# Grouped-query attention on one core: the order model counts the array's switches, and K is turned first in a unit

## The chip, the core and the metric

The kernel runs on one core of a Trainium2 chip. A core has five engines that work side by side and meet through semaphores: TensorE (PE; its weight loads are shown as PEld), VectorE (DVE), ScalarE (ACT), GpSimd (POOL) and SyncE (SP). The metric is device time in microseconds (us), the median of several runs.

## What is computed

Attention in float32 with 8 batches, 512 positions, 32 query heads, 8 key/value heads and a head size of 64; four query heads share a key/value head.

```python
batch, seq, n_heads, n_kv_heads, dim = 8, 512, 32, 8, 64
K_expanded = np.repeat(K, heads_per_group, axis=2)   # also V
scores = np.einsum('bhqd,bhkd->bhqk', Q, K_expanded) * scale
weights = np.exp(scores - np.max(scores, axis=-1, keepdims=True))
weights = weights / (np.sum(weights, axis=-1, keepdims=True) + 1e-10)
output = np.einsum('bhqk,bhkd->bhqd', weights, V_expanded)
return output.transpose(0, 2, 1, 3).astype(np.float32)
```

## The kernel before

**Tiling.** The work is cut into 32 units: a batch and two key/value heads, so eight query heads. A unit has four pairs of query heads. The two heads of a pair use the upper and the lower 64 rows of the PE array at the same time: `mm_scores` (L229) makes, for a pair and a chunk of 128 keys, two matmuls of 64 rows each (the array is row-tiled then) into one PSUM tile of 128 x 1024. A pair has four such chunks. Three of them go to ACT, which takes the exponential (`exp_act`, L245; PSUM tiles `sa`, two buffers). The fourth (chunk 1, `DVE_KC`) goes to DVE, which makes the exponential by an integer trick in one instruction (`exp_dve`, L253; PSUM tile `sd`, one buffer). Both write bf16 weights into `pt`.

**Fills.** Everything else that PE does is a *fill*, and needs all 128 rows of the array. An `out` fill (`mm_out`, L263) multiplies weights by V, with a column of ones beside V that gives the sums: 4 matmuls of 65 columns a block of 128 queries, 7 or 4 blocks a fill. A `turn` fill (`mm_turn`, L322) transposes a unit's Q (two halves of 8) or K (4) on PE. All fills share two PSUM buffers `x`. DVE empties them: `take_out` (L279) copies into `raw`, and after a unit's last block takes the reciprocal of the sums (L303); POOL then divides (L305) and starts the store (L317). `take_turn` (L334) copies into `qt` or `kt`. K's two heads are needed in both halves of the partitions, so behind K's copy SP issues two DMAs that copy each half of `kt` across (L340, L341). The first score of a unit needs both.

**Loads.** POOL issues the loads of Q a unit (L206), and of K and V a batch (L213, L218), cast to bf16 on the way. It runs its own instructions in program order.

**Order.** Nothing is scheduled at run time. `Plan` walks through a model of PE, ACT and DVE with costs for each kind of work and writes down in which order PE and DVE issue theirs. At each step it has three candidates: the next ACT score (time `ta`), the next DVE score (`td`) and the next matmul of the next fill (`tf`). Before, an ACT score is taken when it can start within `LOOK` = 0.05, else a DVE score that can start now, else a fill. The list `fills` (L350 on) sets the order of the fills. In a unit before, they are: out 0, out 7, Q half 0, out 14, Q half 1, out 21, **K**, out 25 (the number is the first block); Q and K are those of two units later. The kernel then replays `plan.ops` (L430 on); loads of the next batch are issued when the scores reach pair 6 of a batch.

Of the kernel before, what the change touches and what calls it, by code (L numbers as in the profile page):

```python
# [19 lines left out]
NEVER = 1e9  # L20


class Plan:

    SCORE, SCORE_LAT = 0.222, 0.436
    BLOCK, TURN, X_LAT = 0.122, 0.056, 0.2
    EXP, EXP_VIS = 0.904, 1.077  # L30
    SCH, SCH_VIS = 1.14, 1.277
    LOOK = 0.05

    def __init__(self, npair, kcs, on_dve, fills, arrive, x_cost, nact, ndve, nx, npt, ahead):
# [5 lines left out]
        parts, x_free = {}, [0.0] * nx  # L40
        ready = []
        pe = act = dve = 0.0
        ia = id_ = fi = at = nxt = 0
        slot = 0

        def have(p):
            u, i = divmod(p, 4)
            return max(parts.get((u, None), NEVER), parts.get((u, i // 2), NEVER))

        def ring(free, issued, n):  # L50
            if issued < n:
                return 0.0
            return free[issued - n] if len(free) > issued - n else NEVER

        def score_at(q, i, free, n):
            if i >= len(q):
                return NEVER
            p = q[i][0]
            if p >= npt and p - npt not in pair_done:
                return NEVER  # L60
            return max(ring(free, i, n), have(p))
# [34 lines left out]
        parts[(0, None)] = parts[(0, 0)] = 0.0  # L96
        while True:
            run_dve(pe)
            ta = score_at(qa, ia, act_free, nact)
            td = score_at(qd, id_, dve_free, ndve)  # L100
            if td < NEVER and ia < len(qa):
                p, kc = qd[id_]
                if p * kcs + kc > qa[ia][0] * kcs + qa[ia][1] + ahead:
                    td = NEVER
            tf = fill_at()
            first = min(ta, td, tf)
            if first > pe and ready:
                soon = min(max(dve, j[0]) for j in ready)
                if soon < first and ta > pe + self.LOOK:
                    pe = max(pe, soon)  # L110
                    run_dve(pe)
                    continue
            if first >= NEVER:
                break
            if ta <= pe + self.LOOK or (first == ta and td > pe and tf > pe):
                pe = max(pe, ta)
                self.ops.append((pe, "pe", "act", qa[ia]))
                start = max(act, pe + self.SCORE_LAT)
                self.ops.append((start, "act", "score", qa[ia]))
                act = start + self.EXP  # L120
                act_free.append(start + self.EXP_VIS)
                pt_done[qa[ia]] = start + self.EXP_VIS
                ia += 1
                pe += self.SCORE
            elif td <= pe or (first == td and tf > pe):
                pe = max(pe, td)
                self.ops.append((pe, "pe", "dve", qd[id_]))
                ready.append((pe + self.SCORE_LAT, "score", qd[id_], None))
                id_ += 1
                pe += self.SCORE  # L130
            else:
                f = fills[fi]
                pe = max(pe, tf)
                self.ops.append((pe, "pe", f[0], (f, at)))
                pe += self.TURN if f[0] == "turn" else self.BLOCK
                if at == 0:
                    slot = nxt % nx
                    x_free[slot] = NEVER
                    nxt += 1
                at += 1  # L140
                if f[0] == "out" and (f[2] + at) % 8 == 0:
                    pair_done[f[1] * 4 + (f[2] + at) // 8 - 1] = pe
                if at == f[3]:
                    ready.append((pe + self.X_LAT, f[0], f, slot))
                    fi, at = fi + 1, 0
        assert ia == len(qa) and id_ == len(qd) and fi == len(fills) and not ready
        self.ops = [o for _, o in sorted(enumerate(self.ops), key=lambda e: (e[1][0], e[0]))]

# [2 lines left out]
def kernel(  # L151
# [14 lines left out]
    NU = B * GP  # L166
# [30 lines left out]
    score, xs = {}, {}  # L197
# [153 lines left out]
    for u in range(NU):  # L351
        if u == 0:
            fills += [("out", 0, 0, 7), ("out", 0, 7, 7), ("turn", 1, 1, 8)]
            fills += [("turn", 2, 0, 8), ("out", 0, 14, 7), ("turn", 2, 1, 8)]
            fills += [("out", 0, 21, 4), ("turn", 2, None, 4), ("out", 0, 25, 7)]
        elif u < NU - 1:
# [8 lines left out]
        else:  # L365
            fills += [("out", u, lo, 4) for lo in range(0, UB, 4)]

    def x_cost(f):
        if f[0] == "turn":
# [6 lines left out]
    def arrive(f):  # L376
        return {(0, 1): 2.0, (1, None): 4.0}.get(f[1:3], 5.0 if f[1] == 1 else 0.0)

    plan = Plan(
        NP, SC, lambda p, kc: kc == DVE_KC, fills, arrive, x_cost,  # L380
        nact=2, ndve=1, nx=2, npt=4, ahead=3,
    )

    with tc.manual_schedule(engines={PE, ACT, DVE, POOL, SP}):
# [45 lines left out]
        for _, engine, kind, what in plan.ops:  # L430
# [4 lines left out]
            elif engine == "pe":  # L435
                p, kc = what
# [42 lines left out]
```

## Time and profile before

| | |
|---|---|
| time, median of 3 runs | 409.66 us (409.02 to 410.01) |
| profiled execution, its own time | 408.85 us |
| its span, first to last instruction | 407.1 us |
| PE busy | 371.7 us (91%) |
| ACT busy | 367.6 us (90%) |
| DVE busy | 302.7 us (74%) |
| POOL busy | 193.0 us (47%) |
| chain that ended last, by engine | PE 65%, DVE 15%, DMA 12% |

Busy time of PE counts matmuls whose ends are modelled, so 91% does not say that PE works at its peak. PE and ACT are about equally busy; which of them holds up the other can't be read from the shares, only from the waits.

### The profile page before, as it was taken

The numbers are of one execution on the slowest core, as the hardware profiler recorded it, in microseconds if no ns is written. First come the engines' busy times: TensorE is split into PE (matmuls) and PEld (weight loads), VectorE is DVE, ScalarE is ACT, GpSimd is POOL, SyncE is SP. The second block draws the span as 40 slices with busy tenths as digits, with TensorE's granted clock in tenths as the row PEclk, the third lists the DMA queues.
The fourth block names the chain that finished last, engine by engine and source line by source line (L and its number), as shares of the span: only waits on it lengthen the run. The fifth ranks groups of instructions, "written<-read, shape, count | busy, mean of one in ns | idle before, by whom it ended". The sixth has DMA issues, their size and how long they took to land.

```text
span 407.1 us, 12995 instructions
## 1 busy us (share of the span) xinstructions
PE 371.7 (91%) x5764; PEld 225.7 (55%) x5764; DVE 302.7 (74%) x426; ACT 367.6 (90%) x387; POOL 193.0 (47%) x135
## 2 busy tenths in 40 slices
PE   4998999998999979999899989999899998999993
PEld 1454556655665535656456645655556564656552
DVE  3775778876787848878778767878678886888872
ACT  3897999997999949999899988999799998999993
POOL 7024544456544545445555652456643357444353
PEclk9998999998999969999999998999999999999998
DMA  9996167769367991678945597655967769422326
GB/s 183 212 177 161 41 163 169 170 157 239 84 134 171 191 236 39 147 169 185 242 131 147 136 202 178 151 147 146 199 146 171 168 149 245 121 68 99 119 105 208
DMA packets 41961, 64.15 MB, mean 158 GB/s; under 512 B 2352, under 2 KB 33968, under 8 KB 41904
## 3 DMA queue, kind: packets, MB, share of 16 engines
q0 software_dynamic: 33776, 57.41, 63.3%
q1 hardware_dynamic: 7600, 5.64, 5.3%
q8 instruction: 45, 0.74, 0.7%
q10 hardware_dynamic: 528, 0.26, 0.2%
q14 instruction: 12, 0.10, 0.1%
HBM read 50.59 MB, written 33.55 MB: 207 GB/s over the span
## 4 chain that ended last, share of the span: by engine, by line
PE 65%; DVE 15%; DMA 12%; issue 3%; ACT 3%; POOL 1%; DVEq 0%; POOLq 0%; ACTq 0%
PE x L270 27%; PE sa L236 22%; DMA kt<-kt 10%; PE x L332 9%; DVE pt L254 9%; PE sd L236 7%; DVE qt L346 4%; DMA q_nat<-in_Q_dram 3%; ACT pt L246 3%; DVE kt L339 1%; DVE raw L290 1%; POOL v_nat L218 0%; POOL q_nat L206 0%; DVEq L254 0%; POOL k_nat L213 0%
## 5 line engine op out<-in xcount | busy, mean ns | idle before, releaser
L246 ACT ACTIVATE pt<-sa 128x1024 bf16<-128x1024 f32 x384 | 365.1, 1029 | 28.1 <-PE sa L236 23.0
L254 DVE TENSOR_SCALAR pt<-sd 128x1024 uint16<-128x1024 f32 x128 | 156.4, 1222 | 70.2 <-PE sd L236 65.0
L305 POOL TENSOR_TENSOR o_sb<-raw,inv 128x2048 f32<-128x2048 f32 (+2 forms) x33 | 115.0, 3485 | 185.6 <-DVE inv L303 185.6
L270 PEld LDWEIGHTS <-pt 128*128 128x128 bf16 x4096 | 147.5, 98 | 63.2 <-issue 61.0
L236 PE MATMUL sa<-qt,kt 64*128 64x512 bf16 x768 | 153.0, 395 | 2.2 <-ACT pt L246 2.0
L290 DVE COPY raw<-x 128x455 f32<-128x455 f32 (+1 forms) x161 | 93.1, 578 | 20.4 <-PE x L270 20.3
L236 PEld LDWEIGHTS <-kt 64*128 64x128 bf16 x1024 | 41.7, 94 | 46.3 <-DMA kt<-kt 14.6
L236 PE MATMUL sd<-qt,kt 64*128 64x512 bf16 x256 | 53.9, 390 | 10.4 <-DMA kt<-kt 10.4
L332 PE MATMUL x<-ident,q_nat 128*128 128x128 bf16 x504 | 50.7, 227 | 0.5 <-DVE raw L290 0.4
L332 PEld LDWEIGHTS <-q_nat 128*128 128x128 bf16 x504 | 31.3, 100 | 33.6 <-issue 32.6
L346 DVE COPY qt<-x 128x1024 bf16<-128x1024 bf16 x63 | 43.0, 682 | 0.9 <-PE x L332 0.7
L317 POOL DMA_DIRECT2D out_dram<-o_sb x31 | 25.2, 813 | 9.3 <-POOL o_sb L305 9.3
L206 POOL DMA_DIRECT2D q_nat<-in_Q_dram x32 | 24.0, 753 | 10.3 <-PE x L332 9.9
L270 PE MATMUL x<-v_155,pt 128*128 128x65 bf16 x512 | 23.8, 197 | 1.5 <-DVE raw L290 1.5
L332 PE MATMUL x<-ident,k_nat 128*128 128x128 bf16 x124 | 16.8, 223 | 8.9 <-DVE qt L346 8.7
L332 PEld LDWEIGHTS <-k_nat 128*128 128x128 bf16 x124 | 9.2, 98 | 26.5 <-issue 26.4
L270 PE MATMUL x<-v_3822,pt 128*128 128x65 bf16 x512 | 23.2, 197 | 0.0
L270 PE MATMUL x<-v_1856,pt 128*128 128x65 bf16 x512 | 23.1, 197 | 0.0
L270 PE MATMUL x<-v_836,pt 128*128 128x65 bf16 x512 | 22.7, 196 | 0.0
L270 PE MATMUL x<-v_6771,pt 128*128 128x65 bf16 x512 | 21.8, 194 | 0.7 <-ACT pt L246 0.7
L270 PE MATMUL x<-v_5788,pt 128*128 128x65 bf16 x512 | 22.4, 194 | 0.0
L270 PE MATMUL x<-v_2839,pt 128*128 128x65 bf16 x512 | 22.4, 194 | 0.0
(42 smaller groups left out, 87.6 us busy)
## 6 DMA issues: line engine op xcount, KB each, us to landing
out_dram<-o_sb POOLq DMA_DIRECT2D x31, 1024.0 KB, 5.7
q_nat<-in_Q_dram POOLq DMA_DIRECT2D x31, 512.0 KB, 8.2
v_nat<-in_V_dram POOLq DMA_DIRECT2D x8, 512.0 KB, 10.8
k_nat<-in_K_dram POOLq DMA_DIRECT2D x8, 512.0 KB, 8.0
kt<-kt SPq DMA_DIRECT2D x62, 64.0 KB, 3.1
out_dram<-o_sb SPq DMA_DIRECT2D x1, 512.0 KB, 4.7
out_dram<-o_sb SPq DMA_DIRECT2D x2, 256.0 KB, 3.4
q_102<-in_Q_dram ACTq DMA_DIRECT2D x1, 256.0 KB, 4.3
```

Source lines behind the costliest of these rows:

```text
L206: nc.gpsimd.dma_start(out=t[:, :, lo * D:hi * D], in_=rows(Q, b, HU * gp + lo, HU * gp + hi))
L236: nc.tensor.matmul(s[:, m, :], kt[u][64 * m:64 * m + 64, 0 if m == g else 1, kc * 128:(kc + 1) * 128], qt[u][64 * m:64 * m + 64, i, :], st ...
L246: nc.scalar.activation(out=pts[p][:, kc, :, :], in_=score.pop((p, kc)), func=mybir.ActivationFunctionType.Exp, scale=float(scale),)
L254: nc.vector.tensor_scalar(out=pts[p][:, kc, :, :].bitcast(U16), in0=score.pop((p, kc)), scalar1=float(A_schr), scalar2=float(B_schr), op0= ...
L270: nc.tensor.matmul(xs[f][:, at * D1:(at + 1) * D1], pts[u * HPG + i][:, kc, m, qc * 128:(qc + 1) * 128], v1[u // GP][:, kc, 2 * (u % GP) + ...
L290: nc.vector.tensor_copy(out=raws[u][:, lo:lo + n, :], in_=x[:, 0:n * D1])
L305: eng.tensor_tensor(out=osbs[u].rearrange("p qc h d -> p h qc d")[:, lo // SC:lo // SC + nh], in0=src[:, :, 0:D].rearrange("p (h qc) d -> ...
L317: eng.dma_start(out=rows(out, b, HU * gp + h0, HU * gp + h1), in_=osbs[u][:, :, h0:h1, :].rearrange("p qc h d -> p qc (h d)"),)
L332: nc.tensor.transpose(xs[f][:, at * 128:(at + 1) * 128], src, ident)
L339: nc.vector.tensor_copy(out=k[:, 0, :], in_=x[:, 0:S])
L346: nc.vector.tensor_copy(out=qt[u][:, 2 * part:2 * part + 2, :], in_=x)
```

## The change

It has four parts.

1. `Plan` charges `DRAIN` = 0.1 whenever PE goes from scores to fills or back (the flag `scoring`).
2. A DVE score is taken only while PE is at scores already, that is right behind an ACT score or ahead of one; it comes to stand alone only when nothing else is left. `LOOK` becomes an argument and is 0.
3. In the model, the two DMAs behind K's copy take 4.0 instead of 2.5.
4. The fills of a unit are now: out 0, **K**, out 7, Q half 0, out 14, Q half 1, out 21, out 25.

```diff
-    LOOK = 0.05
+    DRAIN = 0.1
...
-                        parts[(j[2][1], j[2][2])] = start + vis + (2.5 if j[2][2] is None else 0.0)
+                        swap = 4.0 if j[2][2] is None else 0.0
+                        parts[(j[2][1], j[2][2])] = start + vis + swap
...
-            if ta <= pe + self.LOOK or (first == ta and td > pe and tf > pe):
...
-            elif td <= pe or (first == td and tf > pe):
...
+            if ta <= pe + look or (first == ta and not (scoring and td <= pe)):
+                kind = "act"
+            elif scoring and td <= pe:
+                kind = "dve"
+            elif tf <= pe or first == tf:
+                kind = "fill"
             else:
+                kind = "dve"
+            if kind == "fill":
                 f = fills[fi]
-                pe = max(pe, tf)
+                pe = max(pe + (self.DRAIN if scoring else 0.0), tf)
+                scoring = False
...
+            pe = max(pe + (0.0 if scoring else self.DRAIN), ta if kind == "act" else td)
+            scoring = True
...
+    LOOK = 0.0
...
-            fills += [("out", u, 0, 7), ("out", u, 7, 7)]
-            t = u + 2 < NU
-            fills += [("turn", u + 2, 0, 8)] if t else []
-            fills += [("out", u, 14, 7)]
-            fills += [("turn", u + 2, 1, 8)] if t else []
-            fills += [("out", u, 21, 4)]
-            fills += [("turn", u + 2, None, 4)] if t else []
-            fills += [("out", u, 25, 7)]
...
+        fills += [("out", u, 0, 7)]
+        fills += [("turn", u + 2, None, 4)] if t else []
+        fills += [("out", u, 7, 7)]
+        fills += [("turn", 1, 1, 8)] if u == 0 else []
+        fills += [("turn", u + 2, 0, 8)] if t else []
+        fills += [("out", u, 14, 7)]
+        fills += [("turn", u + 2, 1, 8)] if t else []
+        fills += [("out", u, 21, 4), ("out", u, 25, 7)]
```

What this makes of the order, at three places. First DVE, in the repeating unit, before (`raw` are output copies, 455 columns for 7 blocks and 260 for 4, `kt` and `qt` the copies of turned K and Q, TENSOR_SCALAR the exponential of a DVE score):

```order
L254 TENSOR_SCALAR pt<-sd 128x1024
L290 COPY raw<-x 128x455 x2
L254 TENSOR_SCALAR pt<-sd 128x1024
L346 COPY qt<-x 128x1024
L290 COPY raw<-x 128x455
L254 TENSOR_SCALAR pt<-sd 128x1024
L346 COPY qt<-x 128x1024
L290 COPY raw<-x 128x260
L254 TENSOR_SCALAR pt<-sd 128x1024
L339 COPY kt<-x 128x512
L290 COPY raw<-x 128x455
L303 RECIPROCAL inv<-raw 128x32
```

and the same unit of the changed kernel:

```order
L265 TENSOR_SCALAR pt<-sd 128x1024
L301 COPY raw<-x 128x455
L350 COPY kt<-x 128x512
L265 TENSOR_SCALAR pt<-sd 128x1024
L301 COPY raw<-x 128x455
L357 COPY qt<-x 128x1024
L265 TENSOR_SCALAR pt<-sd 128x1024
L301 COPY raw<-x 128x455
L357 COPY qt<-x 128x1024
L265 TENSOR_SCALAR pt<-sd 128x1024
L301 COPY raw<-x 128x260
L301 COPY raw<-x 128x455
```

K's copy has moved from the end of the unit to its second copy. Behind the last row of the changed unit follow the reciprocal (L314) and the next unit's exponential.

Second, PE in the repeating unit. Before, the DVE score (`sd`) stands behind one ACT score (`sa`); here it is the visit between the two halves of K's transposes:

```order
L332 MATMUL x<-ident,k_nat 128x128
L236 LDWEIGHTS kt
L236 MATMUL sa<-qt,kt 128x512
L236 LDWEIGHTS kt
L236 MATMUL sa<-qt,kt 128x512
L236 LDWEIGHTS kt
L236 MATMUL sd<-qt,kt 128x512
L236 LDWEIGHTS kt
L236 MATMUL sd<-qt,kt 128x512
L332 LDWEIGHTS k_nat
```

In the changed unit one visit to the scores holds an ACT, a DVE and another ACT score before the output matmuls go on:

```order
L247 LDWEIGHTS kt
L247 MATMUL sa<-qt,kt 128x512
L247 LDWEIGHTS kt
L247 MATMUL sa<-qt,kt 128x512
L247 LDWEIGHTS kt
L247 MATMUL sd<-qt,kt 128x512
L247 LDWEIGHTS kt
L247 MATMUL sd<-qt,kt 128x512
L247 LDWEIGHTS kt
L247 MATMUL sa<-qt,kt 128x512
L247 LDWEIGHTS kt
L247 MATMUL sa<-qt,kt 128x512
```

The unit has 12 visits before and 11 after, each between two runs of fills.

Third, POOL, where the loads of K and V of the next batch stand. Before:

```order
L206 DMA q_nat<-in_Q_dram 128x4x512
L305 TENSOR_TENSOR o_sb<-raw,inv 128x8x4x64
L317 DMA out_dram<-o_sb 128x4x512
L213 DMA k_nat<-in_K_dram 128x4x512
L218 DMA v_nat<-in_V_dram 128x4x512
L206 DMA q_nat<-in_Q_dram 128x4x512
```

and in the changed kernel:

```order
L217 DMA q_nat<-in_Q_dram 128x4x512
L224 DMA k_nat<-in_K_dram 128x4x512
L229 DMA v_nat<-in_V_dram 128x4x512
L316 TENSOR_TENSOR o_sb<-raw,inv 128x8x4x64
L328 DMA out_dram<-o_sb 128x4x512
L217 DMA q_nat<-in_Q_dram 128x4x512
```

The two loads have moved ahead of a unit's division and store, behind the Q load of the unit before. SP's order and ACT's are the same in both kernels but for line numbers.

More of the change, by code (lines that the diff above doesn't have):

```diff
@@ L31, with __init__ @@
     SCH, SCH_VIS = 1.14, 1.277
-    LOOK = 0.05
-    def __init__(self, npair, kcs, on_dve, fills, arrive, x_cost, nact, ndve, nx, npt, ahead):
+    DRAIN = 0.1
+    def __init__(self, npair, kcs, on_dve, fills, arrive, x_cost, nact, ndve, nx, npt, ahead, look):
         self.ops = []
@@ L60, in score_at @@
                 return NEVER
-            return max(ring(free, i, n), have(p))
+            u, j = divmod(p, 4)
+            return max(
+                ring(free, i, n), parts.get((u, None), NEVER), parts.get((u, j // 2), NEVER)
+            )
         def fill_at():
@@ L108, in __init__ @@
                 soon = min(max(dve, j[0]) for j in ready)
-                if soon < first and ta > pe + self.LOOK:
+                if soon < first and ta > pe + look:
                     pe = max(pe, soon)
@@ L114, in __init__ @@
                 break
-            if ta <= pe + self.LOOK or (first == ta and td > pe and tf > pe):
[L116 to L124, printed above, removed]
-            elif td <= pe or (first == td and tf > pe):
[L126 to L130, printed above, removed]
-            else:
+            if ta <= pe + look or (first == ta and not (scoring and td <= pe)):
[4 more added lines that the diff above has]
+                kind = "fill"
+            else:
+                kind = "dve"
+            if kind == "fill":
                 f = fills[fi]
-                pe = max(pe, tf)
+                pe = max(pe + (self.DRAIN if scoring else 0.0), tf)
+                scoring = False
                 self.ops.append((pe, "pe", f[0], (f, at)))
@@ L145, in __init__ @@
                     fi, at = fi + 1, 0
+                continue
+            pe = max(pe + (0.0 if scoring else self.DRAIN), ta if kind == "act" else td)
+            scoring = True
+            if kind == "act":
+                self.ops.append((pe, "pe", "act", qa[ia]))
+                start = max(act, pe + self.SCORE_LAT)
+                self.ops.append((start, "act", "score", qa[ia]))
+                act = start + self.EXP
+                act_free.append(start + self.EXP_VIS)
+                pt_done[qa[ia]] = start + self.EXP_VIS
+                ia += 1
+            else:
+                self.ops.append((pe, "pe", "dve", qd[id_]))
+                ready.append((pe + self.SCORE_LAT, "score", qd[id_], None))
+                id_ += 1
+            pe += self.SCORE
         assert ia == len(qa) and id_ == len(qd) and fi == len(fills) and not ready
@@ L350 @@
     fills = [("turn", 0, 1, 8), ("turn", 1, None, 4), ("turn", 1, 0, 8)]
[L351 to L356, printed above, removed]
[L357 to L366 removed]
+    for u in range(NU - 1):
+        t = u + 2 < NU
+        fills += [("out", u, 0, 7)]
[6 more added lines that the diff above has]
+        fills += [("out", u, 21, 4), ("out", u, 25, 7)]
+    fills += [("out", NU - 1, lo, 4) for lo in range(0, UB, 4)]
     def x_cost(f):
@@ L380 @@
         NP, SC, lambda p, kc: kc == DVE_KC, fills, arrive, x_cost,
-        nact=2, ndve=1, nx=2, npt=4, ahead=3,
+        nact=2, ndve=1, nx=2, npt=4, ahead=3, look=LOOK,
     )
```

6 lines of the change are left out of this document (1 added, 5 removed).

## The prediction

> **What bounds the kernel now.** I read first who waits for whom, ScalarE (ACT) first, because it has the most fixed work: 384 exponentials.
>
> ```profile
> ACT pt L246 <- PE sa L236: 23.0, 25, 4.0
> PEld L236 <- DMA kt<-kt: 14.6, 9, 3.2
> PE sd L236 <- DMA kt<-kt: 10.4, 7, 2.7
> PE x L332 <- DVE qt L346: 8.7, 25, 0.4
> ```
>
> Each row is waiter <- releaser: total us, times, longest. ACT is idle 23.0 us, always for scores from TensorE (PE). PE in turn waits for the small DMAs kt<-kt, which copy K's two halves across (I call them the swap), and 25 times, 0.35 us each, for a PSUM buffer x that VectorE (DVE) has yet to empty. Next I cut the ACT row by windows: 94 to 343 us, then 33 to 41 us. The last two fences have the first and last run of exponentials.
>
> ```profile
> ACT pt L246 <- PE sa L236: 16.0, 11, 4.0
> ```
> ```profile
> ACT pt L246 <- PE sa L236: 2.7, 4, 1.3
> ```
> ```profile
> 8.66 2.86 ACT L246 ACTIVATE pt<-sa 128x1024 bf16<-128x1024 f32 x3 [1.26 <-PE sa L236]
> ```
> ```profile
> 341.75 58.84 ACT L246 ACTIVATE pt<-sa 128x1024 bf16<-128x1024 f32 x62 [1.51 <-PE sa L236]
> ```
>
> So 16.0 us are lost in 11 gaps of the main stretch and 2.7 us in four early ones. One such place in the chain that ended last:
>
> ```profile
> 88.38 0.23 PE sd L236 x2
> ```
> ```profile
> 89.85 0.42 DVE kt L339
> 90.28 0.02 issue
> 90.30 5.35 DMA kt<-kt
> 95.65 0.05 issue
> 95.70 0.39 PE sd L236
> ```
> ```profile
> DMA to landing us min/median/max: 1.9/3.3/6.8
> ```
>
> K's transposes end near 88.6, DVE copies them at 89.85, the swap leaves at 90.30, takes 5.35 us, and PE stands until 95.70. Before, six ACT scores lie between the last transpose of a K and the first score that reads it: 6 x 0.957 = 5.7 us (0.957 is 11.49 / 12, below). Minus 1.7 us from transposes to swap (88.6 to 90.30), minus some 0.7 us by which a score runs ahead of its exponential, 3.3 us are left. The median swap takes 3.3 us and the slowest 6.8: it fits or misses by chance of the traffic.
>
> Between the stalls the pace is that of a repeating unit (4 pairs of heads, 12 ACT scores, 4 DVE scores). The same place of it in the chain, two units apart:
>
> ```profile
> 299.80 0.59 PE x L270 x16
> ...
> 322.79 0.60 PE x L270 x16
> ```
>
> 22.99 / 2 = 11.49 us. ACT alone needs less: in the row of 8.66 three exponentials take 2.86 us, and with 1.02 us for the last the step is 0.92 us, 12 x 0.92 = 11.04 a unit. So between stalls PE sets the pace, by its work and one x wait.
>
> **The change, part by part.** *PE's visits to the scores.* I price a visit from PE's own rows.
>
> ```profile
> 156.61 0.39 PE L236 MATMUL sa<-qt,kt 64*128 64x512 bf16 x2
> 156.84 0.38 PE L236 MATMUL sd<-qt,kt 64*128 64x512 bf16 x2
> 157.15 0.54 PE L270 MATMUL x<-v_1856,pt 128*128 128x65 bf16 x12
> 157.62 0.39 PE L236 MATMUL sa<-qt,kt 64*128 64x512 bf16 x2
> ```
> ```profile
> 157.94 0.90 PE L270 MATMUL x<-v_1856,pt 128*128 128x65 bf16 x24
> 158.77 0.39 PE L236 MATMUL sa<-qt,kt 64*128 64x512 bf16 x2
> ```
> ```profile
> 160.03 0.45 PE L332 MATMUL x<-ident,q_nat 128*128 128x128 bf16 x5
> 160.32 0.41 PE L270 MATMUL x<-v_1856,pt 128*128 128x65 bf16 x8
> 160.66 0.39 PE L236 MATMUL sa<-qt,kt 64*128 64x512 bf16 x2
> ```
>
> From start to start: a score alone 0.32 (157.62 to 157.94), two together 0.54 (156.61 to 157.15), so the second costs 0.22. Twelve output matmuls take 0.47 and 24 take 0.83: 0.03 each and 0.11 fixed. Five transposes and eight outputs take 0.63; minus 0.11 and 0.24, a transpose is 0.055. A visit to the scores thus costs 0.32 + 0.11 - 0.22 = 0.21 us beside its scores. Counted in the two orders, the visits fall from 384 to 351. Only eight DVE scores stood alone before, all in the first 100 us; in the repeating unit every one was beside an ACT score already. There the visits fall from 12 to 11, because one now holds three scores (A D A). PE's work in a unit: before 12 x 0.43 + 4 x 0.22 + 128 x 0.03 + 20 x 0.055 = 10.98; the measured 11.49 has 0.36 of x wait (next fence) and 0.15 that I can't place. After: 11 x 0.43 + 5 x 0.22 + 3.84 + 1.10 = 10.77.
>
> *The x wait changes places.* Before, K's transposes wait for the buffer that qt leaves:
>
> ```profile
> 164.21 0.68 DVE L346 COPY qt<-x 128x1024 bf16<-128x1024 bf16 x1
> ```
> ```profile
> 164.94 0.27 PE L332 MATMUL x<-ident,k_nat 128*128 128x128 bf16 x2 [0.36 <-DVE qt L346]
> ```
>
> That wait goes, as K now comes after the first copy of a unit. What is late next? The outputs behind K need the buffer of that first copy, and DVE has a queue ahead of it: last copy of the unit before, reciprocal, a DVE exponential, then the copy.
>
> ```profile
> 392.24 0.35 DVE L303 RECIPROCAL inv<-raw 128x32 f32<-128x32 f32 x1
> 392.51 1.16 DVE L254 TENSOR_SCALAR pt<-sd 128x1024 uint16<-128x1024 f32 x1
> ```
> ```profile
> L290 DVE COPY raw<-x 128x455 f32<-128x455 f32 (+1 forms) x161 | 93.1, 578 | 20.4 <-PE x L270 20.3
> ```
>
> I count from the last output matmul of a unit. DVE: 0.2 until its copy starts (an estimate), 0.63 copy, 0.03, 0.27 to the exponential (392.24 to 392.51), 1.16 for it, 0.62 copy, 0.05 until PE sees the buffer (164.21 + 0.68 = 164.89, to 164.94): free at 2.96. The 0.62 is the 578 ns mean of that row, which mixes two sizes, moved up for the larger. PE: 0.11 + 0.22 + 0.32 + 20 outputs 0.71 + 0.32 + 8 outputs and 3 transposes 0.515 + 0.32 + 0.055 = 2.57. So PE waits about 0.39 there. One wait of 0.36 goes, one of 0.39 comes; the unit is 11.49 - 0.21 + 0.03 = 11.31, say 11.30. ACT's 11.04 stays under it. Bounds: no new wait, and ACT paces at 11.04; or a wait 0.2 larger, and nothing is won, 11.49. I take 11.30, as each number in it is from a row. Some 28 units run so (the last ones have no transposes): 28 x 0.19 = **5.3 us** less.
>
> *K first.* The swap is issued 12 ACT scores ahead of its first use instead of 6: 12 x 0.94 = 11.3 us, minus 1.7 and 0.7, leaves 8.9 us. All 31 swaps of before took 6.8 us or less. But on POOL the change also moves DMAs: in the batch's turn, the loads of K and V now stand ahead of a unit's division and store, behind the Q load of the unit before.
>
> ```profile
> 83.71 0.81 POOL L317 DMA_DIRECT2D out_dram<-o_sb  x1 [0.30 <-POOL o_sb L305]
> 84.52 0.75 POOL L213 DMA_DIRECT2D k_nat<-in_K_dram  x1
> ```
> ```profile
> v_nat<-in_V_dram POOLq DMA_DIRECT2D x8, 512.0 KB, 10.8
> ```
>
> The burst has the same four transfers (store, Q, K, V), one unit earlier. Before, the swap fell 6.6 us into it (83.71 to 90.30). After, K's copy comes some 3.3 us past the end of a unit's outputs, and the store some 5.2 us past it (0.2 + 0.63 + 0.3 + 3.6 division + 0.3, and the issue), so the swap falls about 11.3 + 3.3 - 5.2 = 9.4 us into a burst. V, issued three DMAs of 0.75 us into the burst, lands about 13 us after it begins (2.3 + 10.8). The swap meets its end, and has 8.9 us for it: I cost this at nothing, bounded above by half of the stalls staying. The loads lie earlier, so nothing waits for them; each delays POOL's division by 1.5 us once a batch, under POOL's idle time of several us. SP's queue keeps its order.
>
> What do the stalls cost? The exponentials run from 8.66 to 341.75 + 58.84 = 400.59. At 11.49 / 12 = 0.957 each, 383 steps and 1.02 us would end at 376.2, so 24.4 us are lost, of which the rows show 23.0 - 1.26 = 21.7. Of those, 16.0 + 2.7 belong to K's swaps, and of the other 3.0 I take 1.1 away (the order there is new; the first of them hang on Q's arrival). 19.8 / 21.7 x 24.4 = **22.3 us** less.
>
> Within the lost time PE also runs at half clock:
>
> ```profile
> 243.90:247.30 3.40, 3.40 (x40) 2.27 (x38) 2.46 (x3) 1.22 (x2) 2.47 (x2) 0.50 1.08 345
> ```
> ```profile
> core 0: 407.1 us, clock 0.976
> ```
>
> Columns of the first: window, its length, busy time of PE, PEld, DVE, ACT, POOL, granted clock, DMA share, GB/s. The clock is 0.50 for 3.4 us, in a stretch right behind one of the stalls; over the whole span it is 0.976, so (1 - 0.976) x 407.1 = 9.8 us of clock are lost. I let these dips go with the stalls. The Trainium skill, page "TensorE: Matmul & The Clock Gate", section "Why this matters for your kernels", says that only idle gaps of over about 3 us bring the half clock. No matmul waits over 2.7 us for kt<-kt (the row PE sd above), yet the dips are there, so the trace does not fit that rule; by it the dips would have another cause and stay (rival 4).
>
> *The tail.* Behind the last score stand 72 output matmuls instead of 40: 32 x 0.03 = 0.96 us.
>
> ```profile
> 400.64 1.04 PE L270 MATMUL x<-v_6771,pt 128*128 128x65 bf16 x28 [0.71 <-ACT pt L246]
> ```
>
> PE waits there 0.71 us for the last exponential, which hides part: between 0.25 and 1.0 us more, I take **+0.6**.
>
> Sum: -22.3 - 5.3 + 0.6 = -27.0 us. The profiled execution took 408.85 us (span 407.1, 1.75 around it): 381.85. It lies 0.81 under the median of before, 409.66, so by the median 382.7; I say **383**.
>
> **Rivals.** 1. *ACT paces*: DVE is free sooner than I count and the new x wait hides. 11.04 a unit, 28 x 0.26 = 7.3 us less: **376**. For it: the 0.2 us step is an estimate; against: DVE's queue there is fixed by the order. 2. *The x wait eats the visit*: 0.2 us more, unit 11.49: **388**. A slip of 0.2 us of one DVE instruction does it. 3. *Swaps still miss*: half of the 22.3 us stays: **394**. Against: 8.9 us to 6.8. 4. *The dips stay*, having another cause than the stalls: half of the 9.8 us of clock, as part of it falls into PE's waits, 4.9: **388**. That is what the clock-gate page would lead to. 5. *Slower*: the wait for x behind K grows to over 1.34 us, where 28 x (1.34 - 0.38) = 27 us eat the gain; with 1.5 us a unit it is **414**. It would need another DVE exponential (1.16 us) in that queue, and the order has none there. 6. *No change*: the stalls were not the swap's doing but PE would be held otherwise: **409.7**. Against: DVE's copy, the swap and PE's restart touch within 0.05 us in the chain.
>
> **How the numbers follow.** Forecast 0.55 (its own range 379 to 387), rival 1 0.12, rival 2 0.17, rival 3 0.05, rival 4 0.05, rival 5 0.03, rival 6 0.03. The range takes in rivals 1 and 2 and nearly rival 3: 374 to 393. About 0.3% is what a measurement of this kernel can tell from no change; faster 0.94, within it 0.03, slower 0.03.
>
> **What would show it.** The rows of PE and its loads waiting for kt<-kt should be near nothing, ACT idle for PE under 6 us, no half clock behind 20 us. The unit should be 11.3 us: 11.0 with ACT gapless speaks for rival 1, 11.5 with an x wait over 0.5 for rival 2. PE's wait for the raw copy should come once a unit, near 0.4 us. A swap landing over 8.9 us after its issue would break the forecast.

## The result and the profile after

| | before | after |
|---|---|---|
| time, median | 409.34 us (407.26 to 410.01, 4 runs) | 382.57 us (381.19 to 384.50, 4 runs) |
| ratio of the times | | 0.9357, 95% interval 0.9296 to 0.9419 |
| profiled execution | 408.85 us | 384.50 us |
| its span | 407.1 us | 382.6 us |
| PE, ACT busy | 371.7, 367.6 us | 359.7, 358.5 us |

The changed kernel is 26.8 us (6.5%) faster; forecast were 383.0 us and 27.0 us less. Timed again later against other runs of before (median 406.59), it took 383.03 us, ratio 0.9427 (0.9385 to 0.9469), so 23.6 us less.

First the cores and who waits for whom, after the change (waiter <- releaser: total us, times, longest):

```profile
core 0: 382.6 us, clock 0.994
```
```profile
ACT pt L257 <- PE sa L247: 5.1, 5, 1.8
...
PE x L281 <- DVE raw L301: 3.7, 21, 0.3
...
PE x L343 <- DMA q_nat<-in_Q_dram: 1.9, 2, 0.9
```

No row has PE or its weight loads waiting for kt<-kt (before, PE 10.4 us and its weight loads 14.6, in the same stalls). ACT's idle time for PE fell from 23.0 to 5.1 us, all of it in the first 21 us. The new x wait is there, 0.3 us at most. The mean clock rose from 0.976 to 0.994. The chain that ended last, by engine, and the landing times of the swaps:

```profile
PE 70%; DVE 18%; DMA 3%; issue 2%; POOL 2%; ACT 1%; POOLq 0%; ACTq 0%; DVEq 0%
```
```profile
DMA to landing us min/median/max: 1.9/2.0/5.5
```

DMA's share of the chain fell from 12% to 3%. The swaps themselves land sooner, 2.0 us in the median instead of 3.3. But one swap in each batch, from the second load burst on, still falls into the loads. Here is one such, the same row cut to 166 to 178 us:

```profile
DMA to landing us min/median/max: 4.8/4.9/5.0
```

It leaves at 169.9, some 9 us after that burst began with a store at 160.7, and its two DMAs land in 4.8 and 5.0 us; ones like it took up to 6.8 before.

Then ACT by time. Columns: start, length, engine, line, operation, count, and in brackets the idle time before. A row joins instructions between which the engine rested less than 0.15 us, so its length gives the pace of the exponentials:

```profile
207.09 165.21 ACT L257 ACTIVATE pt<-sa 128x1024 bf16<-128x1024 f32 x177 [0.15 <-ACT pt L257]
```

177 exponentials with hardly a rest: less 1.02 us for the last, 164.19 / 176 = 0.933 us a step, 11.20 us for a unit of 12 (before 11.49). All later units are read from such rows in this way unless another is named. What PE does in the only slow step of a unit:

```profile
219.49 0.39 PE L247 MATMUL sa<-qt,kt 64*128 64x512 bf16 x2
219.81 0.62 PE L343 MATMUL x<-ident,q_nat 128*128 128x128 bf16 x8
220.34 0.53 PE L281 MATMUL x<-v_3756,pt 128*128 128x65 bf16 x12
220.80 0.39 PE L247 MATMUL sa<-qt,kt 64*128 64x512 bf16 x2
```

Between two scores lie all eight transposes of a Q half and twelve output matmuls, 1.31 us from score to score. ACT's exponentials there start 1.17 us apart. Nearly all its other steps, by their starts in the trace, are 0.90 to 0.95 us, and PE begins nine scores in ten 0.05 to 0.3 us after ACT has left their buffer (one in four in experiment 1, which has the old order without its stalls). So ACT seems to pace the unit: 12 x 0.904 = 10.85, and most of the rest is that one step.

Two places got worse. The end of the run, ScalarE's last row being the one above (it ends at 372.30): POOL, SP and DVE.

```profile
367.93 3.61 POOL L316 TENSOR_TENSOR o_sb<-raw,inv 128x2048 f32<-128x2048 f32 x1 [4.50 <-DVE inv L314]
371.83 0.79 POOL L328 DMA_DIRECT2D out_dram<-o_sb  x1 [0.30 <-POOL o_sb L316]
372.65 2.90 POOL L316 TENSOR_TENSOR o_sb<-raw,inv 128x1024 f32<-128x1024 f32 x2
```
```profile
374.59 2.45 SPq L328 DMA_DIRECT2D out_dram<-o_sb  x3
```
```profile
374.59 0.18 DVE L314 RECIPROCAL inv<-x 128x4 f32<-128x4 f32 x1 [0.82 <-POOL o_sb L316]
```

and SP there before:

```profile
399.80 3.12 SPq L317 DMA_DIRECT2D out_dram<-o_sb  x3
```

From the last exponential's end to the span's end it is 382.6 - 372.30 = 10.3 us, before 407.1 - 400.59 = 6.5. SP has issued its last store 4.74 us after that exponential (before 402.92 - 400.59 = 2.33), and from there to the end it takes 5.6 us (before 4.2). PE's output matmuls end only 0.2 us later, measured so: 370.86 + 2.76 = 373.62 is 1.32 us behind the exponential, 1.12 before. What is late is POOL, which divides and stores the whole unit 30 until 372.62 and has both of its divisions of the last unit still ahead; DVE's last reciprocal waits 0.82 us for the first of them.

The other place is the start, where the first twelve exponentials take 15.25 us instead of 13.45. The chain of waits cut to 8 to 24 us has the load of Q, before and after:

```profile
3.85 10.72 DMA q_nat<-in_Q_dram
```
```profile
3.85 12.48 DMA q_nat<-in_Q_dram
```

It lands 1.8 us later after, which looks like the cause. The same kernel in experiment 12 says otherwise. There the load is almost as late, yet the twelve take 13.67. What differs is the clock: PE's scores at that place, after, and in experiment 12:

```profile
18.43 0.61 PE L247 MATMUL sa<-qt,kt 64*128 64x512 bf16 x2
...
19.83 0.39 PE L247 MATMUL sa<-qt,kt 64*128 64x512 bf16 x2
```
```profile
3.85 12.26 DMA q_nat<-in_Q_dram
```
```profile
14.57 0.66 PE L247 MATMUL sd<-qt,kt 64*128 64x512 bf16 x2
...
16.43 0.39 PE L247 MATMUL sa<-qt,kt 64*128 64x512 bf16 x2
```

A score takes 0.61 us at the half clock of the start and 0.39 at full clock, which begins at 19.6 us after and at 15.2 in experiment 12 (15.2 before, too). Over the fourteen profiles of this study, the twelve exponentials take 12.6 to 13.7 us where full clock begins at 13.4 to 15.2 us, and 15.0 to 16.0 where it begins at 19.3 to 21.1. Kernels of both kinds are in either group.

### The profile page after: what moved, and what is told of

It is laid out like the page before. It is cut to its first block, busy times and chain, and to the rows that moved or that the text cites. A ratio compares the mean times of both kernels' runs of the same rounds, so it can differ in the third digit from the quotient of the medians.

```text
span 382.6 us, 12995 instructions
## 1 busy us (share of the span) xinstructions
PE 359.7 (94%) x5764; PEld 226.9 (59%) x5764; DVE 305.3 (80%) x426; ACT 358.5 (94%) x387; POOL 192.3 (50%) x135
## 4 chain that ended last, share of the span: by engine, by line
PE 70%; DVE 18%; DMA 3%; issue 2%; POOL 2%; ACT 1%; POOLq 0%; ACTq 0%; DVEq 0%
PE x L281 32%; PE sa L247 23%; DVE pt L265 9%; PE x L343 9%; DVE raw L301 8%; PE sd L247 6%; DMA q_nat<-in_Q_dram 3%; ACT pt L257 1%; POOL o_sb L316 1%; POOLq L480 0%; DVE inv L314 0%; POOL v_nat L229 0%; POOL out_dram L328 0%; POOL q_nat L217 0%; POOL k_nat L224 0%
## 5 line engine op out<-in xcount | busy, mean ns | idle before, releaser
L257 ACT ACTIVATE pt<-sa 128x1024 bf16<-128x1024 f32 x384 | 356.0, 1058 | 8.9 <-PE sa L247 5.1
L281 PEld LDWEIGHTS <-pt 128*128 128x128 bf16 x4096 | 149.9, 98 | 83.3 <-issue 82.1
L265 DVE TENSOR_SCALAR pt<-sd 128x1024 uint16<-128x1024 f32 x128 | 154.8, 1209 | 40.6 <-PE sd L247 35.1
L247 PE MATMUL sa<-qt,kt 64*128 64x512 bf16 x768 | 150.4, 390 | 0.3 <-ACT pt L257 0.3
L247 PEld LDWEIGHTS <-kt 64*128 64x128 bf16 x1024 | 44.9, 94 | 31.7 <-issue 2.4
L247 PE MATMUL sd<-qt,kt 64*128 64x512 bf16 x256 | 49.9, 386 | 0.0
L343 PE MATMUL x<-ident,q_nat 128*128 128x128 bf16 x504 | 40.4, 223 | 1.9 <-DMA q_nat<-in_Q_dram 1.9
L343 PEld LDWEIGHTS <-q_nat 128*128 128x128 bf16 x504 | 28.9, 99 | 17.5 <-issue 14.2
L217 POOL DMA_DIRECT2D q_nat<-in_Q_dram x32 | 24.0, 753 | 12.6 <-PE x L343 11.9
L281 PE MATMUL x<-v_155,pt 128*128 128x65 bf16 x512 | 23.6, 195 | 1.4 <-DVE raw L301 1.2
L281 PE MATMUL x<-v_3756,pt 128*128 128x65 bf16 x512 | 23.1, 194 | 0.7 <-DVE raw L301 0.3
L281 PE MATMUL x<-v_2773,pt 128*128 128x65 bf16 x512 | 23.1, 194 | 0.6 <-DVE raw L301 0.3
L281 PE MATMUL x<-v_1790,pt 128*128 128x65 bf16 x512 | 23.1, 194 | 0.6 <-DVE raw L301 0.5
L281 PE MATMUL x<-v_807,pt 128*128 128x65 bf16 x512 | 23.1, 194 | 0.6 <-DVE raw L301 0.3
L281 PE MATMUL x<-v_5722,pt 128*128 128x65 bf16 x512 | 23.1, 194 | 0.6 <-DVE raw L301 0.3
L281 PE MATMUL x<-v_4739,pt 128*128 128x65 bf16 x512 | 23.1, 194 | 0.6 <-DVE raw L301 0.5
L281 PE MATMUL x<-v_6705,pt 128*128 128x65 bf16 x512 | 22.3, 194 | 0.6 <-DVE raw L301 0.3
## 6 DMA issues: line engine op xcount, KB each, us to landing
k_nat<-in_K_dram POOLq DMA_DIRECT2D x8, 512.0 KB, 10.3
```

The costliest lines, as they stand in the source:

```text
L217: nc.gpsimd.dma_start(out=t[:, :, lo * D:hi * D], in_=rows(Q, b, HU * gp + lo, HU * gp + hi))
L247: nc.tensor.matmul(s[:, m, :], kt[u][64 * m:64 * m + 64, 0 if m == g else 1, kc * 128:(kc + 1) * 128], qt[u][64 * m:64 * m + 64, i, :], st ...
L257: nc.scalar.activation(out=pts[p][:, kc, :, :], in_=score.pop((p, kc)), func=mybir.ActivationFunctionType.Exp, scale=float(scale),)
L265: nc.vector.tensor_scalar(out=pts[p][:, kc, :, :].bitcast(U16), in0=score.pop((p, kc)), scalar1=float(A_schr), scalar2=float(B_schr), op0= ...
L281: nc.tensor.matmul(xs[f][:, at * D1:(at + 1) * D1], pts[u * HPG + i][:, kc, m, qc * 128:(qc + 1) * 128], v1[u // GP][:, kc, 2 * (u % GP) + ...
L343: nc.tensor.transpose(xs[f][:, at * 128:(at + 1) * 128], src, ident)
```

## The experiments

Ratios are to the kernel before, in runs on the same chip. Line numbers shift by a few between the kernels.

**1. Before without the swap's result.** The two DMAs go into a tile that nobody reads, and both heads of a pair read K's straight copy. So half of the scores use the wrong half of K.

```diff
...
-                kt[u][64 * m:64 * m + 64, 0 if m == g else 1, kc * 128:(kc + 1) * 128],
+                kt[u][64 * m:64 * m + 64, 0, kc * 128:(kc + 1) * 128],
...
-            nc.sync.dma_start(out=k[64:128, 1, :], in_=k[0:64, 0, :])
-            nc.sync.dma_start(out=k[0:64, 1, :], in_=k[64:128, 0, :])
+            kx = kx_pool.tile([128, S], BF16, name="kx")
+            nc.sync.dma_start(out=kx[64:128, :], in_=k[0:64, 0, :])
+            nc.sync.dma_start(out=kx[0:64, :], in_=k[64:128, 0, :])
```

> The kernel before, same order on every engine; the two swap DMAs are still issued, but into a tile that nobody reads, and both matmuls of a score read K's straight copy (so the swapped half of K is left out of the scores). Theory S (the stalls are the swap's landing, and the half-clock dips follow from them): about 22 us less than before, 387 (385 to 390), no row of PE or its loads waiting for a kt DMA, ACT idle for PE under 6 us in all, no half clock after 20 us. Rival D (the dips have a cause of their own): about 392, dips still there. Rival N (PE would be held otherwise, by DVE or the loads): 405 to 409.

391.05 us, ratio 0.9611 (0.954 to 0.9682), 1 us above the expected range. Cores, ACT by time, and a wait:

```profile
core 0: 389.7 us, clock 0.998
```
```profile
58.21 325.02 ACT L247 ACTIVATE pt<-sa 128x1024 bf16<-128x1024 f32 x339 [0.67 <-PE sa L237]
```
```profile
PE x L333 <- DVE qt L348: 9.3, 26, 0.4
```

The span falls by 17.4 us, though the start is 2.3 us slower here. The unit stays: 324.00 / 338 x 12 = 11.50. So the stalls cost some 17 to 20 us, all of them hang on the swap, and the clock's dips go with them. The old x wait of 0.36 a unit stays, as it should.

**2. K first alone**, the order's rules of before with the fills of after (part 4 of the change).

```diff
...
-            fills += [("turn", u + 2, None, 4)] if t else []
-            fills += [("out", u, 25, 7)]
...
+        fills += [("out", u, 0, 7)]
+        fills += [("turn", u + 2, None, 4)] if t else []
+        fills += [("out", u, 7, 7)]
...
+        fills += [("out", u, 21, 4), ("out", u, 25, 7)]
```

> The old planner with the new list of fills: K is turned 13 to 14 ACT scores ahead of its use, but the visits to the scores are 409 instead of 384 (before) or 351 (after), and 32 DVE scores stand alone. Theory S with 0.21 us a visit: the swap's stalls go as in the first kernel, -22 us; in the repeating unit 13 visits instead of 12 add 0.21 us, the old x wait of 0.36 goes and another may come: 386 to 393, unit 11.3 to 11.7 us. Rival P (the planner's new rules make the gain, K's place little): 400 or more.

394.39 us, ratio 0.9715 (0.9656 to 0.9774), 1.4 us above the expected range.

```profile
38.81 237.96 ACT L246 ACTIVATE pt<-sa 128x1024 bf16<-128x1024 f32 x244 [0.23 <-PE sa L236]
```

The stalls are gone but for one of 0.6 us. The unit is 236.94 / 243 x 12 = 11.70: with K at that place the old rules make 13 visits to the scores instead of 12, with a DVE score alone in each unit, and the unit is 0.21 longer. That is one visit by the price in the prediction, though not cleanly: PE's x wait changes too, from 0.35 us 25 times behind qt to 0.25 us 28 times behind raw.

**3. The order's rules alone**, after with the fills of before (parts 1 to 3); the diff is experiment 2's, reversed.

> The new planner with the old list of fills: 352 visits as after, but only 4 to 6 ACT scores between a K and its use. Theory S: a slack of 4 leaves 3.8 - 2.4 = 1.4 us for a swap of 2 to 3.3, of 5 leaves 2.4, so nearly all units stall, some by 1 to 2 us, and the bursts by more: 402 to 420, PE waiting over 20 us for kt DMAs. Rival P (the planner's rules make the gain): under 392.

396.76 us, ratio 0.9797 (0.971 to 0.9883): below the expected 402 to 420.

```profile
PEld L247 <- DMA kt<-kt: 10.5, 8, 2.1
...
PE sa L247 <- DMA kt<-kt: 8.2, 7, 1.9
```
```profile
270.79 44.48 ACT L257 ACTIVATE pt<-sa 128x1024 bf16<-128x1024 f32 x48 [2.11 <-issue]
```

The stalls are back: PE itself waits 8.2 us for the swap, as against 10.4 before (the weight loads' row covers the same stalls). Between them the unit is 43.46 / 47 x 12 = 11.10, shorter than after's own 11.20. So the rules alone already bring the unit near ACT's pace, which the expectation had not reckoned with, and both parts are needed: alone they save 13.5 (experiment 2) and 11.2 us of the 407.92 that before took in these runs, together 24.7, about what the whole change saves. Parts 2 and 3 were not tried apart.

**4. No charge for the switch**, after with `DRAIN` = 0 (parts 2 to 4).

```diff
-    DRAIN = 0.1
+    DRAIN = 0.0
```

> The changed kernel with DRAIN 0 in the model, so without the knowledge of the drain; the rule that a DVE score goes only beside other scores stays, and K stays first. Its order has 348 visits, 11 in the repeating unit, 16 ACT scores from K to its use, and 40 output matmuls behind the last score instead of 72. Theory V (time goes by visits and the swap's slack, not by the term DRAIN): unit 11.1 to 11.4 us, and POOL's divisions at the end come earlier, so 377 to 383. Rival M (the drain term is what makes the order good): 386 or more.

385.0 us, ratio 0.9473 (0.9417 to 0.9528).

```profile
268.33 107.10 ACT L257 ACTIVATE pt<-sa 128x1024 bf16<-128x1024 f32 x114 [0.80 <-ACT pt L257]
```

The unit is 106.08 / 113 x 12 = 11.27, and 375.43 to the span's end of 381.8 is a tail of 6.4 us. By the starts of the exponentials, number 12 to the last take 352.5 us, in after 347.2. So the charge wins 5.3 us and gives 3.9 back in the tail, and the ratio can't be told from the changed kernel's. The time speaks clearly for neither theory.

**5. The reciprocal later.** A unit's reciprocal, division and store are issued behind the first copy of the next unit, so that DVE frees x sooner for the outputs behind K.

```diff
-            if lo + n == UB:
-                divide(u, 0, UB, nc.gpsimd)
-                store(u, 0, UB, nc.gpsimd)
+            if u > 0 and lo == 0:
+                divide(u - 1, 0, UB, nc.gpsimd)
+                store(u - 1, 0, UB, nc.gpsimd)
...
```

> The changed kernel with a unit's reciprocal, division and store moved behind the next unit's first output copy, so that on DVE the exponential no longer stands behind the reciprocal. Theory X (PE's wait for x behind K comes from that queue on DVE): the exponential starts 0.27 us earlier, the wait falls from 0.3 to under 0.1 us, the unit from 11.20 to 10.95 to 11.05 us, 4 to 7 us in all; POOL's last whole division starts about 1 to 2 us later in the tail: 377 to 381. Rival A (ACT sets the pace by now, the wait is free): unit stays 11.15 to 11.2, 382 to 385.

384.12 us, ratio 0.9457 (0.9401 to 0.9513): no gain.

```profile
207.25 165.49 ACT L257 ACTIVATE pt<-sa 128x1024 bf16<-128x1024 f32 x177 [0.15 <-ACT pt L257]
```

The wait of PE for raw falls from 3.7 us (21 times) to 1.4 (4), and the unit stays at 164.47 / 176 x 12 = 11.21. The x wait is real and costs nothing; the theory that it sets the unit falls.

**6 and 7. The tail.** Unit 30 is divided and stored in two halves; 7 adds 5's edit.

```diff
+            if u == NU - 2:
+                if lo in (14, 25):
+                    a = 0 if lo == 14 else 2 * BLK
+                    divide(u, a, 2 * BLK, nc.gpsimd)
+                    store(u, a, 2 * BLK, nc.gpsimd)
-            if lo + n == UB:
+            elif lo + n == UB:
```

> The changed kernel with the next to last unit divided and stored in two halves, the first after its fill of block 14. Theory T (the tail grew to 10.5 us because POOL's last whole division and its 1 MB store now end behind the last exponential): POOL is free 1.5 to 2 us earlier and half of the store leaves 3 us earlier, so 1.5 to 3 us less, 379.5 to 381. Rival B (the three last stores themselves set the end): 382 to 383.

> The reciprocal behind the next unit's first copy, and the next to last unit in two halves. If X and T both hold: 375 to 378. If only T: 380 to 381. If only X: 377 to 379.

380.60 us, ratio 0.9386 (0.9329 to 0.9443), and 379.98 us, 0.9365 (0.9318 to 0.9411), close to what the tail alone was expected to give. ACT's last row and SP's in 6, whose span is 381.0:

```profile
42.49 330.63 ACT L257 ACTIVATE pt<-sa 128x1024 bf16<-128x1024 f32 x354 [0.36 <-ACT pt L257]
```
```profile
374.91 2.09 SPq L333 DMA_DIRECT2D out_dram<-o_sb  x3
```

The tail is 381.0 - 373.12 = 7.9 us instead of 10.3 with the same 72 output matmuls behind the last score. So 2.4 of the 3.8 us came from POOL's whole division and its store of 1 MB; the edit halves both, so it does not tell them apart.

**8. K's and V's loads at pair 8 instead of 6**, so that they stand behind a store as they did before the change.

```diff
-                    if r == 6:
+                    if r == 8:
                         load_k(b + 1)
```

> The changed kernel with the loads of the next K and V issued at pair 8 of a batch instead of 6, which puts them behind a unit's division and store and ahead of the Q load, as in the kernel before. Theory S (12 scores of slack cover the swap wherever the burst lies): the swap's median landing may rise from 2.0 us, no wait for a kt DMA, 381 to 384. Rival L (the loads' new place took the traffic away from the swap and made the gain): waits for kt DMAs come back, 387 or more.

387.70 us, ratio 0.9533 (0.9466 to 0.96), and by neither theory's cause. The waits, then POOL and PE by time around one stall:

```profile
PEld L343 <- DMA k_nat<-in_K_dram: 6.8, 8, 1.7
DVE kt L350 <- PE x L343: 6.0, 8, 1.7
...
PE x L343 <- DMA k_nat<-in_K_dram: 4.2, 6, 1.6
```
```profile
174.67 0.75 POOL L224 DMA_DIRECT2D k_nat<-in_K_dram  x1
```
```profile
181.50 0.41 PE L281 MATMUL x<-v,pt 128*128 128x65 bf16 x8
183.51 0.34 PE L343 MATMUL x<-ident,k_nat 128*128 128x128 bf16 x3 [1.60 <-DMA k_nat<-in_K_dram]
...
184.39 0.39 PE L247 MATMUL sa<-qt,kt 64*128 64x512 bf16 x2
184.62 0.53 PE L247 MATMUL sd<-qt,kt 64*128 64x512 bf16 x2
...
185.63 0.61 PE L247 MATMUL sa<-qt,kt 64*128 64x512 bf16 x2
```

The swaps are as quick as in after (2.0 us in the median). But K is now turned so early in a unit that its load is not there: issued at 174.67, it is needed at 181.9 and lands by 183.5. K first needs the earlier loads; the change gets them because its order reaches pair 6 ahead of the division. Behind this wait of 1.6 us scores also go from 0.39 to 0.61 us: the granted clock is 0.50 from 184.7 to 188.1, the only such dip of this run after its start and before its end.

**9. No long fill run**: K behind two output fills, the Q halves further back.

```diff
-        fills += [("out", u, 0, 7)]
+        fills += [("out", u, 0, 7), ("out", u, 7, 7)]
         fills += [("turn", u + 2, None, 4)] if t else []
-        fills += [("out", u, 7, 7)]
...
+        fills += [("out", u, 14, 7), ("out", u, 21, 4)]
         fills += [("turn", u + 2, 0, 8)] if t else []
-        fills += [("out", u, 14, 7)]
+        fills += [("out", u, 25, 7)]
         fills += [("turn", u + 2, 1, 8)] if t else []
-        fills += [("out", u, 21, 4), ("out", u, 25, 7)]
```

> Changed kernel, only the order of the fills of a unit differs (out 0-7, out 7-14, K, out 14-21, Q0, out 21-25, Q1), so that no fill run is as long as Q's turn together with eight output matmuls. Theory A (ACT paces the unit and only the longest fill run makes it late: the one step of 1.17 us in a unit goes): unit 10.95 to 11.1 against 11.20, time 376 to 380. Theory P (TensorE's own work sets the unit, ACT only looks gapless): unit 11.2, time 382 to 385, more output matmuls being left behind the last score. If swaps are late again (9 scores' slack at 2 to 6 us landing), rows of waits for kt come back.

394.35 us, ratio 0.969 (0.9633 to 0.9748): both theories missed. PE, then ACT:

```profile
222.55 0.30 PE L281 MATMUL x<-v,pt 128*128 128x65 bf16 x4
222.68 0.39 PE L343 MATMUL x<-ident,k_nat 128*128 128x128 bf16 x4
223.57 0.40 PE L281 MATMUL x<-v,pt 128*128 128x65 bf16 x8 [0.50 <-DVE raw L301]
223.90 0.61 PE L247 MATMUL sa<-qt,kt 64*128 64x512 bf16 x4
```
```profile
216.40 7.48 ACT L257 ACTIVATE pt<-sa 128x1024 bf16<-128x1024 f32 x8
224.38 8.36 ACT L257 ACTIVATE pt<-sa 128x1024 bf16<-128x1024 f32 x9 [0.49 <-ACT pt L257]
```

Now the end of one fill, all of K's turn and the start of a third fall into one gap between scores. The third has to wait 0.50 us for a buffer, with the next score behind it, and ACT stands for 0.49 us once a unit; by the starts of its exponentials the unit is 11.60 us. So an x wait does cost its full length where no score is ready ahead of it. The prediction's rival 2 was a real mechanism; it just has no such place in the changed kernel.

**10. Another order and the split.** After with 6's edit, `DRAIN` = 0.08 and `LOOK` = 0.03, which leaves 52 output matmuls behind the last score.

> Changed kernel with a drain of 0.08 and a look of 0.03 in the order's model, and unit 30 divided and stored in halves. Theory: K keeps its slack, fewer output matmuls are left behind the last score (52 against 72), the division of unit 30 ends earlier; unit 11.1 to 11.2, tail 8 against 10.5: 376 to 380. Rival: the order's model hardly matters here and only the split counts: 380 to 381, as the run with the split alone.

380.56 us, ratio 0.9355 (0.9318 to 0.9393): in the rival's range and not in the theory's. Cores, and ACT's last row:

```profile
core 0: 378.8 us, clock 0.994
```
```profile
206.31 165.33 ACT L257 ACTIVATE pt<-sa 128x1024 bf16<-128x1024 f32 x177 [0.16 <-ACT pt L257]
```

The unit is 11.20 again (164.31 / 176 x 12), the tail 378.8 - 371.64 = 7.2 us, 0.7 less than with the split alone.

**11. Less work for PE**: of the four output matmuls of a block, the third is left out in the second, fourth and sixth block of each output fill, so some keys' part lacks in the output.

```diff
         for kc in range(SC):
+            if kc == 2 and at in (1, 3, 5):
+                continue
```

> Changed kernel in the same order, but the third of the four output matmuls is left out in the second, fourth and sixth block of every output fill: 14 fewer in a unit, 0.42 us less work for TensorE at 0.03 us each (the output lacks these keys' part). Theory A (ACT paces the unit, 12 x 0.904 = 10.85 us, and TensorE only makes the one step late that stands behind the run of eight transposes and twelve, now eleven, outputs): unit 11.10 to 11.18 against 11.20, time 379 to 382. Theory P (TensorE's work sets the unit): the 0.3 us above ACT's floor goes, unit 10.85 to 10.9, time 372 to 375.

379.0 us, ratio 0.934 (0.9276 to 0.9405).

```profile
39.46 327.99 ACT L257 ACTIVATE pt<-sa 128x1024 bf16<-128x1024 f32 x354 [0.33 <-ACT pt L257]
```

326.97 / 353 x 12 = 11.12: with 0.42 us less work for PE the unit is only 0.08 shorter. ACT paces.

**12. The changed kernel again**, to compare with 6, 7 and 10.

> The changed kernel itself once more, to place the runs with the split tail, which were timed against other runs of before. If the split is worth the 2.4 us that its traces show: 382 to 384 and a ratio of 0.940 to 0.944, above the 0.9365 and 0.9355 of the two kernels with it. If it is worth nothing: the same 380 and 0.936.

383.03 us, ratio 0.9427 (0.9385 to 0.9469). The versions with the split tail have 0.9386, 0.9365 and 0.9355, 0.4 to 0.7% below, with intervals that all touch this one, and the first timing of the changed kernel had 0.9357. So the times alone do not show that they are faster. What shows it are the traces: from exponential 12 to the last all of them take 347 us, as the changed kernel does, and their tails are at least 2.3 us shorter.

## Why the prediction came out right

The time was right to 0.5 us; the terms were not, and that they largely cancel is luck: the order brought 5.2 us more than forecast, the stalls 2.6 less, and the tail took 3.2 and the start 1.8 more. The table sums the starts of the exponentials, numbered from 0, in the traces of before, of experiment 1 (before without stalls) and of after:

| stretch | before | experiment 1 | after |
|---|---|---|---|
| exponential 0 to 12 | 13.45 | 15.79 | 15.25 |
| 12 to 96 | 89.66 | 83.74 | 79.29 |
| 96 to 360 | 266.41 | 252.65 | 246.73 |
| 360 to 383 (the last) | 21.32 | 21.30 | 21.14 |
| end of the last to the span's end | 6.5 | 6.4 | 10.3 |

From 12 on, the second column less the first gives the stalls, the third less the second the order.

| term | predicted | measured |
|---|---|---|
| stalls by K's swap | -22.3 | -19.7 |
| order, a shorter unit | -5.3 | -10.5 |
| tail | +0.6 | +3.8 |
| start | 0 | +1.8 |
| sum | -27.0 | -24.6 (the span fell by 24.5; the last exponential itself takes 0.1 longer) |

The profiled execution thus came out some 2.5 us slower than the sum; the median, 382.57, does not, since the other runs of after spread down to 381.19. The later timing, 23.6 us less, falls 3.4 short of the sum.

**The stalls** were named rightly. K first takes them away (experiment 2) and the order's rules alone don't (3). They are worth 2.6 us less than the share of the lost time that the prediction gave them ("19.8 / 21.7 x 24.4"). The step "it fits or misses by chance of the traffic" was wrong: in the trace of before, the seven waits of PE of over 0.8 us come once for each of the seven later K loads, at the swap that leaves about 6 us after that load's issue. These swaps land in 5.1 to 6.8 us, all others but the first in at most 4.0. And a unit's first score needs only the first of the two DMAs, not both: in the prediction's chain it has landed at 95.65 and PE goes on at 95.70, while the second lands at 96.77.

**The dips of the clock** went with the stalls, so rival 4 is out: 0.998 in experiment 1. They follow gaps between PE's matmuls that are shorter than 3 us: 0.9 to 2.7 before the change, 1.6 in experiment 8. The Trainium skill's rule ("TensorE: Matmul & The Clock Gate", "Why this matters for your kernels": no idle gaps of over about 3 us between bursts of matmuls), taken as the prediction takes it, that only such gaps bring the half clock, does not agree with these traces.

**The unit** was put at 11.30 and is 11.20, but the step behind it failed: PE was to set the pace after the change as well, and "ACT's 11.04 stays under it". The floor was read from the first three exponentials (0.92 us a step), and the steps in the stretch are 0.904 in the median, so it is 10.85. The visit saved and a PE that runs ahead of ACT leave ACT in charge, with one late step a unit. Experiments 5 and 11 show it: neither a shorter x wait nor less PE work moves the unit by more than 0.08. That is rival 1's mechanism, at a unit that lies between its own 11.04 and the forecast's. The x wait behind K was foreseen at 0.39 and came at up to 0.3, but under ACT's pace.

The larger half of the mis-sized term lies elsewhere: the first seven units from exponential 12 on gained 4.45 us, 0.64 each, where later ones gain 5.92 / 22 = 0.27. The prediction saw that the old order has eight DVE scores alone in the first 100 us and still priced only the repeating unit. By the two traces the first seven units lose 13 visits and the later ones one each; at the prediction's 0.21 us a visit this gives an estimate of 2.7 of the 4.45 us and 4.6 of the 5.92. That the visits are the cause is argued from the order; no run takes them apart.

**The tail** failed: "between 0.25 and 1.0 us more" counted PE's output matmuls, which do add only 0.2 us. What ends the span is the stores. POOL's division of unit 30 now ends beside the last exponential, the last divisions queue behind it, and three stores go out late beside a store of 1 MB. Experiment 6, with unit 30's division and store in halves, gets 2.4 us of it back, and experiment 10, with fewer outputs left over, 0.7 more; the rest stays open.

**The loads** were costed at nothing because "the loads lie earlier, so nothing waits for them". True, but they had to be earlier: two pairs later, experiment 8 waits for K and loses about 1% against the changed kernel. The meeting of the swap with the end of a burst came as foreseen, in six of the seven bursts behind the start: the swap of 169.9 leaves some 9 us into its burst (9.4 in the prediction), and such swaps land in 4.8 to 5.5 us. The slack of 8.9 us covers them, so costing this at nothing was right.

**The start** was not in the sum. The load of Q is later after, but experiment 12 shows the same kernel with such a load and a quick start; the time goes with the moment at which the clock first becomes full. Why that is some 5 us later in some executions, no run shows.

## What to carry to other kernels

When a wait is taken away, find out anew which engine paces the stretch, from its step in a long gapless run and not from its first few instructions: here it passed from PE to ACT, and from then on less work for PE bought almost nothing. Moving a consumer forward moves the deadline of its load as well. And at the end of a program, follow the last result to its store on every engine; the matmuls behind the last score cost 0.2 us here, a late division and the stores behind it 3.6.

## What the hardware showed unexpectedly

Short waits can cost twice. Of the seven gaps of over 0.8 us between PE's matmuls in the trace of before, from 20 us on, three (0.9, 1.3 and 1.5 us) are followed within 2.5 us by half clock (0.50) for 3.4 us. In the longest (2.7 us) it sets in before the gap ends and lasts 6.8 us. After the others (1.0, 1.2, 1.7) the clock stays full. Experiment 3 has six such gaps of 0.8 to 1.9 us and one dip, behind the longest. The waits of 0.5 us once a unit in experiment 9 brought none.

The first half clock of a run can end at 13.4 or at 21.1 us of its span with nearly the same program, and the first unit takes up to 3.4 us longer for it (experiments 7 and 6). That is more than several of the changes tried here are worth, so the spans of single executions can't be compared without looking at it.

A 64 KB copy between partitions lands in 1.9 to 6.8 us in the trace of before, and in up to 7.5 in experiment 3's, by what else is moving.
